# A shared ring of six small buffers for the key choice's maxima in a hybrid attention step

## The chip, the cores and the metric

The kernel runs on one core of a Trainium2 chip. The time is the device time of one execution in microseconds (us). Five engines work in parallel, each through its own queue in order: TensorE (PE, matmuls and transposes), VectorE (DVE), ScalarE (ACT), GpSimd (POOL) and SyncE (SP), which here only issues transfers. An instruction that waits holds up all that stand behind it in the queue of its engine.

## The reference

One step of a streaming encoder layer over 576 tokens: 512 of a prompt and 64 of a sample, which also sees 128 cached ones. The input is projected once; the columns belong to two groups of eight heads each. The first group is attention with a forget gate, the second is sparse attention: each query may only use the keys that an indexer chooses.

```python
def dsa_attend(q, k, v, iq, ik, iw, q_pos, k_pos, topk):
    logits = jnp.einsum('bqhd,bld->bqhl', iq, ik, preferred_element_type=jnp.float32)
    score = jnp.einsum('bqh,bqhl->bql', iw.astype(jnp.float32), jax.nn.relu(logits))
    admissible = (k_pos[None, :] // CHUNK) <= (q_pos[:, None] // CHUNK)
    score = jnp.where(admissible[None], score, NEG)
    _, sel = lax.top_k(score, topk)
    ...
    s = jnp.einsum('bqhd,bqkhd->bhqk', q, kg, preferred_element_type=jnp.float32) * HEAD_DIM ** -0.5
    p = jax.nn.softmax(jnp.where(valid[:, None], s, NEG), axis=-1)
```

`topk` is 128 for the prompt and 48 for the sample. Then come an output projection, a layer norm, a feed-forward part of width 4096 with a squared ReLU, a second layer norm, and a gated addition. All of it is in float32.

## The kernel before, in words

**Tiling.** Tokens lie along the free dimension, and 1024 features are eight tiles of 128 rows. Each float32 product is three matmuls of a rounded type, high by high, high by low and low by high; ACT makes the high half of every weight tile (L183), DVE or POOL the low half (L187). The heads are taken in eight pairs, 0 to 3 with the forget gate and 4 to 7 sparse. While the scores of pair p are worked off, PE projects pair p+1 (L279); both are mixed into one stream.

**Score jobs.** A pair has nine jobs: four blocks of 128 queries for each of two heads, with 128, 256, 384 and 512 keys, and one for the sample with both heads and 192 keys. A job runs through stages in successive ticks: `qk` (PE, L817, L824, L826) into a PSUM tile S; `addmax` (DVE, L834) adds the bias and takes the row's extreme into column 0 of a small tile `st`; `exp` (ACT, L842) reads it as its bias; for the sample job `norm` puts a sum and its reciprocal into `st` (L847, L848) and takes the reciprocal of the pair's sums (L850), which ACT spreads into `rows` (L852); `ptrans` transposes on PE; `pevac` copies to PT (ACT, L890, for pairs 0 to 3, DVE, L892, after that); `pv` (L912) multiplies with the values once for a whole pair. S, T and X share three PSUM banks, so a late reader of one of them stops PE.

**Key choice.** In pair 0 the indexer's logits are made (PE L611, ACT L616 into four buffers `work`, DVE L619 and L621 into `dbias`). A generator, `choice`, then runs rounds: the eight largest values of each row (`DVE.max`, L641) are replaced by a very small number (`match_replace`, L643, which the profile shows as a value load and a replacement). 16 rounds make 128 keys for each of the query blocks 1 to 3 (`dbias_97`, `dbias_98`, `dbias_99`, with 256, 384 and 512 keys), 6 rounds make 48 for the sample (`dbiasS`). An activation (L645) then turns what is left into a bias. Pair 4's jobs are the first that need it.

**What sets the order.** The source emits the instructions in one stream; after each step of the main loop a filler, `choose`, draws from `choice` at a fixed rate. The recording layer then reorders: an instruction may go ahead of earlier ones on its engine if its operands are ready by the layer's own estimate. A tile from a ring of `bufs` buffers can be written only after its buffer's last owner, `bufs` allocations ago in the source, has been read; so allocations of one ring stay in their order. The maxima lie in `m8`, one tile with two halves that rounds use in turn and that has no part in any ring. The statistics of the jobs lie in a ring `st` of four buffers.

Of the kernel before, what the change touches and what calls it, by code (L numbers as in the profile page):

```python
# [8 lines left out]
F32 = mybir.dt.float32  # L9
# [27 lines left out]
def tile_hybrid_step(ctx: ExitStack, tc: tile.TileContext, I, O):  # L37
# [249 lines left out]
    sb = pA.enter_context(tc.tile_pool(name="sb", bufs=1))  # L287
# [29 lines left out]
    cS = sb.tile([8, PAST + NS], F32, name="cS")  # L317
    dbiasS = sb.tile([128, PAST + NS], F32, name="dbiasS")
    iw = sb.tile([128, 5, 8], F32, name="iw")
    m8 = sb.tile([128, 2, 8], F32, name="m8")  # L320


    def tiles_of(name, k):
# [191 lines left out]
    def idx_rest():  # L515
        ACT.copy(ZkT[:, NP:NP + PAST], kiraw)
        DVE.tensor_tensor(ZkT[64:128, NP:NP + PAST], kiraw[64:128], f(ZkT[64:128, NP:NP + PAST]), OP.subtract)
        made = deque()
        for b0, nb in ((0, 2), (2, 2), (4, 1)):
            idx_rope(b0, nb)  # L520
            yield 1
            for b in range(b0, b0 + nb):
                for make, move in [zk_stack(b)] + ([zq_stack(b, hh) for hh in range(2)] if b else []):
                    make()
                    made.append(move)
                    if len(made) > 2:
                        made.popleft()()
                    yield 1
        done.add(0)
        while made:  # L530
            made.popleft()()
            yield 1
        SP.dma_start(O["ki"].rearrange("p (b d) -> p b d", b=5), idxs[:, :, 256:288])
# [68 lines left out]
    def logit_jobs():  # L602
        for i in range(1, 5):
            n, nk = (128, (i + 1) * 128) if i < 4 else (NS, PAST + NS)
            k0 = 0 if i < 4 else NP
            dst = dbias[i] if i < 4 else dbiasS
            while i not in done or (i < 4 and len(done) < i + 1):
                yield 0.5
            for h in range(8):
                ps = psum_1("SX"[h % 2], 1)  # L610
                PE.matmul(ps[:n, :nk], ZqT[:, h, (i - 1) * 128:(i - 1) * 128 + n], ZkT[:, k0:k0 + nk],  # L611
                          start=True, stop=True)
                r = work[:, h % 4 * 512:h % 4 * 512 + 512]

                def ev(h=h, n=n, nk=nk, i=i, ps=ps, r=r, dst=dst):
                    ACT.activation(r[:n, :nk], ps[:n, :nk], AF.Relu)  # L616
                    w = iw[:n, i, h:h + 1]
                    if h == 0:
                        DVE.tensor_scalar(dst[:n, :nk], r[:n, :nk], w, None, op0=OP.mult)  # L619
                    else:  # L620
                        DVE.scalar_tensor_tensor(dst[:n, :nk], r[:n, :nk], w, dst[:n, :nk], op0=OP.mult, op1=OP.add)  # L621
                later(LG, ev)
                yield nk / 960 + 0.1

    def choice():
        for _ in idx_rest():
            yield 0.6
        yield from logit_jobs()
        state["logits"] = True
        for _ in range(4):  # L630
            yield 0.5
        POOL.memset(dbias[0], 0.0)
        POOL.memset(dbias[0][0:64, 64:128], -NEG)
        for i in range(1, 5):
            n = 128 if i < 4 else NS
            s = dbias[i] if i < 4 else dbiasS[:NS]
            if i < 4:
                DVE.memset(s[0:64, i * 128 + 64:(i + 1) * 128], NEG)
            for r in range(16 if i < 4 else 6):
                m = m8[:n, r % 2]  # L640
                DVE.max(m, s)  # L641
                yield s.shape[1] / 960 + 0.1
                DVE.match_replace(out=s, in_to_replace=m, in_values=s, imm_value=GONE)  # L643
                yield s.shape[1] / 960 + 0.1
            ACT.activation(s, s, AF.Relu, bias=big[:n, 0:1])  # L645
            if i == 4:
                ACT.copy(dbiasS[64:128], dbiasS[0:64])
            state["chosen"] = i
            yield 0.4
# [179 lines left out]
    def addmax(j):  # L829
        n = j["S"].shape[1]  # L830
        t = sb.tile([128, 512], F32, name="sP", bufs=4)
        st = sb.tile([128, 4], F32, name="st", bufs=4)
        j["P"], j["st"] = t[:, :n], st
        DVE.tensor_tensor_reduce(j["P"], j["S"], j["bias"], scale=1.0, scalar=-GONE, op0=OP.add, op1=OP.min,  # L834
                                 accum_out=st[:, 0:1])
# [92 lines left out]
    def jobs_of(p):  # L928
        out = [dict(p=p, hh=hh, i=i, s=False, close=i % 2 == 1 and hh == 1) for i in range(4) for hh in range(2)]
        return out + [dict(p=p, s=True, close=True)]  # L930

    PLAN = (((oevac, 5), (addmax, 1), (exp, 2), (make_bias, 0), (make_bias, -1)),
            ((ptrans, 3), (norm, 2)),
            ((qk, 0), (pevac, 3), (scales, 3), (pv, 4)))
# [59 lines left out]
    drive(idx_main(), 24, None, 0)  # L994
    n_proj = 24
    state["choice"] = choice()
    bg = bg0()
    next(bg)
# [564 lines left out]
```

## Time and profile before

| What | Value |
|---|---|
| Median of three runs | 794.18 us (794.14 to 794.25) |
| Profiled execution, whole | 795.54 us |
| Its span, first to last instruction | 793.8 us |
| PE busy | 780.9 us, 98% |
| PE weight loads busy | 759.0 us, 96% |
| DVE busy | 539.4 us, 68%, 1100 instructions |
| ACT busy | 434.0 us, 55% |
| POOL busy | 119.4 us, 15% |
| Granted TensorE clock | 0.999 |
| MAX8 of the blocks, of the sample | 48 and 6 |

Busy times come from the profile's first part. A matmul's end is modelled, so PE's busy time is not PE at its peak. In a row of a timeline stand the start, the duration, the engine, the source line, the operation, the tiles written and read with their shapes, and in brackets the idle time ahead of it and who ended it. In a row of the view by stretches stand the stretch, its length, and busy time with instruction count for each engine.

### The profile page before, as it was taken

How to read it: one execution, taken by the hardware profiler on the slowest of the kernel's cores; microseconds unless marked ns; L12 is line 12 of the kernel's file. 1: busy time of each engine (PE TensorE's matmuls, PEld its weight loads, DVE VectorE, ACT ScalarE, POOL GpSimd, SP SyncE). 2: the span in 40 equal slices, each digit the busy share in tenths (PEclk: the TensorE clock that was granted, in tenths of full speed). 3: DMA queues.
4: the chain of work that ended last, by engine and by line, in shares of the span. 5: the costliest groups of instructions: out<-in, count | busy, mean ns of one | idle time of the engine just before them, and what ended most of it. 6: DMA issues, size and time to landing. Idle time of an engine off the chain costs nothing.

```text
span 793.8 us, 14800 instructions
## 1 busy us (share of the span) xinstructions
PE 780.9 (98%) x5822; PEld 759.0 (96%) x5822; DVE 539.4 (68%) x1100; ACT 434.0 (55%) x912; POOL 119.4 (15%) x121
## 2 busy tenths in 40 slices
PE   9999899999999999999999999999999999999997
PEld 8988798899999999999999999999999999999997
DVE  7679999653556655989846749477494765647653
ACT  5468666787777645587415426254362534626451
POOL 8103244454242000110000000000000000012200
PEclk9999999999999999999999999999999999999999
DMA  8537132344222233341214223042231413631001
GB/s 299 195 41 168 58 105 92 100 157 144 89 85 86 72 99 112 150 152 64 97 54 130 83 65 120 30 136 78 82 105 32 156 54 107 244 108 35 28 27 67
DMA packets 31127, 81.44 MB, mean 103 GB/s; under 512 B 5073, under 2 KB 10193, under 8 KB 30929
## 3 DMA queue, kind: packets, MB, share of 16 engines
q1 hardware_dynamic: 30768, 80.27, 31.8%
q8 instruction: 46, 0.75, 0.4%
q10 hardware_dynamic: 288, 0.22, 0.1%
q14 instruction: 25, 0.20, 0.1%
HBM read 66.38 MB, written 9.54 MB: 96 GB/s over the span
## 4 chain that ended last, share of the span: by engine, by line
PE 80%; DVE 10%; issue 5%; ACT 2%; POOL 1%; DMA 1%; SPq 0%; DVEq 0%; ACTq 0%; POOLq 0%
PE g L279 55%; PE m L279 13%; PE n L279 2%; DVE dbias L643 2%; DVE m L641 2%; PE V L912 2%; PE T L65 1%; DVE dbias L621 1%; PE m L422 1%; PE X L65 1%; PE m L429 1%; PE S L826 1%; PE S L429 1%; PE S L824 1%; DVE sP L834 1%
## 5 line engine op out<-in xcount | busy, mean ns | idle before, releaser
L183 ACT CAST whl<-wraw 128x512 fp32r<-128x512 f32 (+1 forms) x226 | 134.9, 611 | 168.9 <-PE g L279 145.1
L279 PE MATMUL g<-BH,whl 128*128 128x288 f32 (+2 forms) x864 | 181.6, 297 | 0.5 <-DVE Y L1218 0.5
L279 PE MATMUL m<-AH,whl 128*128 128x288 f32 x736 | 177.9, 308 | 0.0
L187 DVE TENSOR_TENSOR whl<-wraw,whl 128x512 fp32r<-128x512 f32 (+1 forms) x192 | 130.1, 697 | 68.2 <-ACT whl L183 67.4
L279 PEld LDWEIGHTS g<-BH,whl 128*128 128x128 f32 x864 | 141.1, 188 | 2.7 <-ACT u L1327 1.1
L279 PEld LDWEIGHTS m<-AH,whl 128*128 128x128 f32 x736 | 126.3, 188 | 1.9 <-issue 1.0
L279 PE MATMUL g<-BL,whl 128*128 128x288 f32 (+2 forms) x432 | 127.3, 295 | 0.0
L279 PE MATMUL m<-AL,whl 128*128 128x288 f32 x368 | 109.0, 296 | 0.0
L279 PE MATMUL g<-hidE,whl 128*128 128x288 f32 (+2 forms) x768 | 103.4, 295 | 0.0
L279 PE MATMUL g<-hidO,whl 128*128 128x288 f32 (+2 forms) x768 | 103.3, 295 | 0.0
L279 PEld LDWEIGHTS g<-hidO,whl 128*128 128x128 f32 x768 | 102.3, 188 | 0.0
L279 PEld LDWEIGHTS g<-hidE,whl 128*128 128x128 f32 x768 | 102.2, 188 | 0.1
L279 PEld LDWEIGHTS g<-BL,whl 128*128 128x128 f32 x432 | 81.3, 188 | 0.2
L279 PEld LDWEIGHTS m<-AL,whl 128*128 128x128 f32 x368 | 69.5, 189 | 0.7
L279 PE MATMUL g<-s,whl 128*128 128x288 f32 x432 | 68.4, 298 | 0.0
L279 PEld LDWEIGHTS g<-s,whl 128*128 128x128 f32 x432 | 60.0, 188 | 2.2 <-DVE u L1329 1.2
L1108 POOL TENSOR_TENSOR ln_s<-Y 128x576 f32<-128x576 f32 (+2 forms) x3 | 4.4, 1469 | 381.6 <-DVE Y L1393 369.2
L842 ACT ACTIVATE sP<-sP,st 128x128 f32<-128x128 f32 (+4 forms) x72 | 39.6, 550 | 35.4 <-DVE st L834 35.2
L187 POOL TENSOR_TENSOR whl<-wraw,whl 128x512 fp32r<-128x512 f32 x34 | 44.2, 1301 | 81.9 <-ACT whl L183 46.6
L1368 DVE SCALAR_TENSOR_TENSOR Y<-Y,g 128x576 f32<-128x576 f32 x48 | 36.0, 751 | 21.6 <-PE g L279 21.2
L279 PE MATMUL m<-BH,whl 128*128 128x288 f32 x192 | 43.4, 304 | 0.0
L183 ACT CAST whl<-wsum 128x512 fp32r<-128x512 f32 x24 | 14.8, 617 | 32.9 <-PE g L279 32.7
(282 smaller groups left out, 1263.9 us busy)
## 6 DMA issues: line engine op xcount, KB each, us to landing
wraw<-in_w_up_dram SPq DMA_DIRECT2D x32, 512.0 KB, 3.5
wraw<-in_w_down_dram SPq DMA_DIRECT2D x32, 512.0 KB, 3.5
wraw<-in_w_qkv_dram SPq DMA_DIRECT2D x23, 512.0 KB, 3.6
wraw<-in_w_gate_dram SPq DMA_DIRECT2D x8, 512.0 KB, 4.4
wraw<-in_w_o_dram SPq DMA_DIRECT2D x8, 384.0 KB, 3.1
out_vT_dram<-v SPq DMA_DIRECT2D x8, 288.0 KB, 2.1
Y<-in_xT_dram SPq DMA_DIRECT2D x8, 288.0 KB, 4.4
PLD<-PL SPq DMA_DIRECT2D x4, 576.0 KB, 3.5
```

The source lines that it names most:

```text
L65: PE.transpose(out, in_, ident[:n, :n])
L183: ACT.copy(self.hv[h][0], src)
L187: eng.tensor_tensor(lv, src, f(hv), OP.subtract)
L279: PE.matmul(ps, W(w, kw, wc), a[:, ka, cols], start=(first and i == 0), stop=(last and i == n - 1))
L422: PE.matmul(mk[:, h, :HW], w0(part, k), a[:, k, h * HW:(h + 1) * HW], start=(k == 0 and i == 0), stop=(k == 7 and i == 2))
L429: PE.matmul(acc[b][:n[b], :304], a[:, k, b * 128:b * 128 + n[b]], ixw(part, k), start=(k == 0 and i == 0), stop=(k == 7 and i == 2))
L621: DVE.scalar_tensor_tensor(dst[:n, :nk], r[:n, :nk], w, dst[:n, :nk], op0=OP.mult, op1=OP.add)
L641: DVE.max(m, s)
L643: DVE.match_replace(out=s, in_to_replace=m, in_values=s, imm_value=GONE)
L842: ACT.activation(j["P"], j["P"], AF.Exp, bias=j["st"][:, 0:1], scale=-1.0, accum_out=s)
L912: PE.matmul(P["O"][r, (i - 1) * 128 + c.start:(i + 1) * 128], P["vt"][:, kb, r], t[:, hh, kb, c], start=(kb == 0), stop=(kb == i))
L1368: later(0, lambda y=y, m=m, s=s: DVE.scalar_tensor_tensor(y, y, s, m[:, :, :HW], op0=OP.mult, op1=OP.add))
```

## The change

`m8` is gone. A round takes its maxima's tile from the ring `st`, whose tiles now have eight columns and of which there are six. Score jobs take theirs from the same ring. Nothing else is edited; below the edit, line numbers are 3 higher (L641 becomes L644, L834 becomes L837).

```diff
-    m8 = sb.tile([128, 2, 8], F32, name="m8")
...
+    def stats():
+
+        return sb.tile([128, 8], F32, name="st", bufs=6)
+
...
-                m = m8[:n, r % 2]
+                m = stats()[:n]
                 DVE.max(m, s)
...
-        st = sb.tile([128, 4], F32, name="st", bufs=4)
+        st = stats()
```

The order on PE and on POOL stays as it was. On DVE the rounds stand elsewhere. The first place is the end of pair 0 on DVE, where the last weighted sums of the logits (`dbiasS<-work`) are made; `ISA sP,st` is `addmax`, and `m_105` is the tile `m8`. Before:

```order
L621 SCALAR_TENSOR_TENSOR dbiasS<-work,iw,dbiasS 64x192
L643 MATCH_REPLACE dbias_97<-m_105,dbias_97 128x256
L621 SCALAR_TENSOR_TENSOR dbiasS<-work,iw,dbiasS 64x192
L850 RECIPROCAL sums<-sums 128x8
L641 MAX m_105<-dbias_97 128x8
L621 SCALAR_TENSOR_TENSOR dbiasS<-work,iw,dbiasS 64x192
L643 MATCH_REPLACE dbias_97<-m_105,dbias_97 128x256
L621 SCALAR_TENSOR_TENSOR dbiasS<-work,iw,dbiasS 64x192
```

Now:

```order
L620 SCALAR_TENSOR_TENSOR dbiasS<-work,iw,dbiasS 64x192 x2
L853 RECIPROCAL sums<-sums 128x8
L620 SCALAR_TENSOR_TENSOR dbiasS<-work,iw,dbiasS 64x192 x3
L837 ISA sP,st<-S,biasS 128x192
L837 ISA st 128x1
L620 SCALAR_TENSOR_TENSOR dbiasS<-work,iw,dbiasS 64x192
L850 RECIPROCAL st<-st 128x1
L837 ISA sP,st<-S,causal 128x128
L837 ISA st 128x1
L644 MAX st<-dbias_97 128x8
```

No round stands between the weighted sums any more; the first one comes behind pair 1's first job. The second place is DVE around the third job of pair 1, the first with 256 keys. Before:

```order
L834 ISA sP,st<-S,causal 128x128
L834 ISA st 128x1
L643 MATCH_REPLACE dbias_97<-m_105,dbias_97 128x256
L641 MAX m_105<-dbias_97 128x8
L641 MAX m_105<-dbias_98 128x8
L643 MATCH_REPLACE dbias_97<-m_105,dbias_97 128x256
L643 MATCH_REPLACE dbias_98<-m_105,dbias_98 128x384
L641 MAX m_105<-dbias_98 128x8
L834 ISA sP,st<-S,causal 128x256
```

Now:

```order
L644 MAX st<-dbias_97 128x8
L646 MATCH_REPLACE dbias_97<-st,dbias_97 128x256
L837 ISA sP,st<-S,causal 128x256
L837 ISA st 128x1
L644 MAX st<-dbias_97 128x8
L646 MATCH_REPLACE dbias_97<-st,dbias_97 128x256
L927 TENSOR_TENSOR mix_1357<-V,mix_1357 128x512
L837 ISA sP,st<-S,causal 128x256
```

Before, the 16 rounds of the 256 keys ended ahead of this job; now it stands behind six of them. The third place is DVE at the end of pair 3, with the rotary products of the next pair's queries (`x`, `xr`, `qE`, `qO`). Before:

```order
L834 ISA sP,st<-S,causal 128x512
L834 ISA st 128x1
L721 SCALAR_TENSOR_TENSOR x_2209<-m,cosT 128x576
L722 TENSOR_TENSOR xr<-xr,sinT 128x576
L723 TENSOR_TENSOR x_2209<-x_2209,xr 128x576
L834 ISA sP,st<-S,causal 128x512
L834 ISA st 128x1
L727 TENSOR_TENSOR qE<-x_2209,qE 64x576
L728 TENSOR_TENSOR qO<-x_2209,qO 64x576
L850 RECIPROCAL sums<-sums 128x8
L834 ISA sP,st<-S,biasS 128x192
```

Now:

```order
L837 ISA st 128x1
L724 SCALAR_TENSOR_TENSOR x_2248<-m,cosT 128x576
L725 TENSOR_TENSOR xr<-xr,sinT 128x576
L644 MAX st<-dbias_99 128x8
L726 TENSOR_TENSOR x_2248<-x_2248,xr 128x576
L646 MATCH_REPLACE dbias_99<-st,dbias_99 128x512
L837 ISA sP,st<-S,causal 128x512
L837 ISA st 128x1
L730 TENSOR_TENSOR qE<-x_2248,qE 64x576
L731 TENSOR_TENSOR qO<-x_2248,qO 64x576
L644 MAX st<-dbias_99 128x8
L853 RECIPROCAL sums<-sums 128x8
```

No round stood in pair 3 behind its second job; now the rounds of the 512 keys do, and the last rounds of the sample stand in pair 4, ahead of its seventh job.

## The prediction

> **What bounds the kernel now.** I read the chain of waits first, to see which engine the end hangs on.
>
> ```profile
> ## 4 chain that ended last, share of the span: by engine, by line
> PE 80%; DVE 10%; issue 5%; ACT 2%; POOL 1%; DMA 1%; SPq 0%; DVEq 0%; ACTq 0%; POOLq 0%
> ```
>
> TensorE (PE) carries most of it, but a tenth of the chain, some 79 us, lies on VectorE (DVE). The view by stretches shows where. I cut it at the starts of the value products of the head pairs, the 24 matmuls of L912, because they come once per pair:
>
> ```profile
> L912 PE MATMUL V<-PT,vtok x24: 272/379/430, 95.8 to 97.9; 128*64 128x256 f32 x16, 128*64 128x128 f32 x8
> L912 PE MATMUL V<-PT,vtok x24: 272/379/430, 126.3 to 128.4; 128*64 128x256 f32 x16, 128*64 128x128 f32 x8
> L912 PE MATMUL V<-PT,vtok x24: 272/379/430, 155.7 to 157.8; 128*64 128x256 f32 x16, 128*64 128x128 f32 x8
> L912 PE MATMUL V<-PT,vtok x24: 272/379/430, 184.0 to 186.1; 128*64 128x256 f32 x16, 128*64 128x128 f32 x8
> L912 PE MATMUL V<-PT,vtok x24: 272/379/430, 212.3 to 214.4; 128*64 128x256 f32 x16, 128*64 128x128 f32 x8
> ```
>
> ```profile
> core 0: us, PE busy (x) PEld busy (x) DVE busy (x) ACT busy (x) POOL busy (x), PEclk, DMA share, GB/s
> 60.00:86.00 26.00, 23.57 (x160) 21.32 (x159) 25.70 (x69) 21.67 (x58) 7.46 (x7) 1.00 0.55 128
> 86.00:95.80 9.80, 8.93 (x71) 8.32 (x68) 9.42 (x34) 4.51 (x14) 1.29 (x1) 1.00 0.26 85
> 95.80:126.30 30.50, 29.20 (x222) 27.24 (x221) 29.55 (x85) 19.55 (x51) 12.92 (x11) 1.00 0.34 101
> 126.30:155.70 29.40, 28.82 (x224) 27.30 (x223) 24.95 (x75) 21.33 (x55) 15.42 (x14) 1.00 0.35 105
> 155.70:184.00 28.30, 28.30 (x224) 27.20 (x223) 10.95 (x30) 24.09 (x58) 13.54 (x11) 1.00 0.51 169
> 184.00:212.30 28.30, 28.30 (x222) 27.23 (x221) 14.24 (x38) 21.39 (x50) 11.74 (x9) 1.00 0.27 91
> ```
>
> From 60 to 126 us DVE is busy 97 to 99% of the time, and PE takes 30.50 us for 222 matmuls that take it 28.30 us later. The next pair takes 29.40 us for the 224 that take 28.30 us after it. So a full DVE costs PE 2.2 and 1.1 us in these two steps. Before 95.8 us there is no undisturbed twin to compare with; PE's recorded idle time is 2.43 + 0.87 = 3.3 us. Altogether about 6.6 us of PE time are lost while the key choice runs, and from 155.7 us, when its rounds are over, nothing.
>
> Trace Analysis of the Trainium skill (Identifying the Most-Contended Engine) says that matmul busy time judges PE badly, because matmuls are pipelined, and weight-load busy time judges it better. By matmul busy time the two steps would lose only 1.30 + 0.58 = 1.9 us; by weight loads the share is 89% and 93% against 96% later, which is 3.2 us, and the trace's own step lengths side with that.
>
> The waits of PE themselves, in the timeline:
>
> ```profile
> 74.69 0.50 PE L824 MATMUL S<-kE,qE 128*128 128x512 f32 x1 [0.47 <-ACT PT L890]
> 84.76 0.59 PE L817 MATMUL S<-KcT,QB 128*128 128x192 f32 x2 [1.57 <-ACT PT L890]
> 94.35 0.39 PE L824 MATMUL S<-kE,qE 128*128 128x256 f32 x1 [0.56 <-DVE st L834]
> 95.17 0.66 PE L65 MATMUL X<-ident,rows 128*128 128x128 f32 x4 [0.31 <-ACT VS L774]
> 124.93 0.39 PE L824 MATMUL S<-kE,qE 128*128 128x256 f32 x1 [0.70 <-DVE st L834]
> ```
>
> Two name DVE. Those that name ScalarE (ACT) go back to DVE too, as the largest shows:
>
> ```profile
> 82.13 0.20 ACT L842 ACTIVATION_READ_ACCUMULATOR sP<-sP,st 128x1 f32 x1
> 83.50 0.18 DVE L850 RECIPROCAL sums<-sums 128x8 f32<-128x8 f32 x1
> 83.72 0.62 ACT L852 COPY rows<-sums 128x512 f32<-128x512 f32 x1 [0.97 <-DVE sums L850]
> ```
>
> The sums were ready at 82.33 us, the reciprocal ran 1.17 us later behind rounds and weighted sums, ACT's copy waited for it, and behind that copy in ACT's queue stood the copy of PT for which PE waited 1.57 us.
>
> **The change part by part.** Removed: one tile. Added: nothing that executes. The number of rounds is the same, 48 + 6, and PE's and POOL's orders are word for word the old ones apart from buffer numbers; on SP one load of Y passes one store. Moved: the rounds on DVE, and with them ACT's four activations and one copy that turn finished rounds into biases. One round is a MAX8, a value load and a MATCH_REPLACE8, and its pitch is the distance of two MAX8 with nothing between:
>
> ```profile
> 90.72 0.43 DVE L641 MAX8 m<-dbias 128x8 f32<-128x256 f32 x1
> 91.70 0.43 DVE L641 MAX8 m<-dbias 128x8 f32<-128x256 f32 x1
> 103.71 0.56 DVE L641 MAX8 m<-dbias 128x8 f32<-128x384 f32 x1
> 104.96 0.56 DVE L641 MAX8 m<-dbias 128x8 f32<-128x384 f32 x1
> 121.67 0.69 DVE L641 MAX8 m<-dbias 128x8 f32<-128x512 f32 x1
> 123.18 0.69 DVE L641 MAX8 m<-dbias 128x8 f32<-128x512 f32 x1
> ```
>
> So 0.98, 1.25 and 1.51 us for 256, 384 and 512 keys. A pair's jobs begin some 6 us before its step as cut above (89.53 for pair 1, below); I take the two as one. In the new order no round stands before pair 1's first score job; then some 16 + 2 rounds (256, 384) fall into pair 1, 14 + 1 (384, 512) into pair 2, 11.5 of 512 into pair 3, and the rest into pair 4.
>
> *The logit stage, 60 to 95.8 us.* In 60 to 86 us the two instructions of a round took, MAX8 first:
>
> ```profile
> 60.00:86.00 26.00, 3.32 (x8) 1.00 0.55 128
> 60.00:86.00 26.00, 3.82 (x16) 1.00 0.55 128
> ```
>
> That is 7.1 us of 26 that leave: DVE's 25.70 falls to 18.6. The 1.17 us of the late reciprocal go; of the 0.47 I count 0.2, because ACT's own queue has a part in it. The 0.56 at 94.35 came from this:
>
> ```profile
> 89.53 0.28 DVE L834 CUSTOM_DVE_ANT_0 sP<-S,causal 128x128 f32<-128x128 f32 x1
> 94.02 0.27 DVE L834 CUSTOM_DVE_ANT_0 sP<-S,causal 128x128 f32<-128x128 f32 x1
> 94.33 0.40 ACT L842 ACTIVATE sP<-sP,st 128x128 f32<-128x128 f32 x1 [3.02 <-DVE st L834]
> ```
>
> Between pair 1's first two score jobs 4.49 us of DVE work stood; now there are three rounds, 3 x 0.98 + 0.28 = 3.2 us. I count 0.5 of 0.56 and 0.2 of 0.31. Sum 2.1 us; bounds 1.2 (the reciprocal alone) and 3.3 (all recorded idle).
>
> *Pair 1, 95.8 to 126.3 us.* 16 x 0.98 + 2 x 1.25 = 18.2 us of rounds, and the other instructions take at most the 10.95 us of the third step, which has the rotary products on top: clearly under 29.2, where DVE held 29.55 before, and in narrow rounds, behind which a score job waits less. Of 2.2 us lost I count 1.9 back, bounds 1.1 and 2.2.
>
> *Pair 2.* 14 x 1.25 + 1.51 = 19.0 us of rounds in a step of 28.3, again beside 4 to 11 us. Of 1.1 lost, 0.8 back, bounds 0.4 and 1.1.
>
> *Pair 3, new load.* 11.5 x 1.51 = 17.4 us join 10.95 us: 28.3 of 28.3. Here DVE is full where it was 39% busy. The worst place is the pair's end, which ran like this:
>
> ```profile
> 168.85 0.69 DVE L834 CUSTOM_DVE_ANT_0 sP<-S,causal 128x512 f32<-128x512 f32 x1 [1.81 <-ACT whl L183]
> 171.91 0.69 DVE L834 CUSTOM_DVE_ANT_0 sP<-S,causal 128x512 f32<-128x512 f32 x1
> 175.28 0.20 DVE L850 RECIPROCAL sums<-sums 128x8 f32<-128x8 f32 x1 [1.04 <-ACT sP L842]
> 175.40 0.36 DVE L834 CUSTOM_DVE_ANT_0 sP<-S,biasS 128x192 f32<-128x192 f32 x1
> ```
>
> One round now stands between the first two rows, which have no idle time between them: the second comes 1.5 us late. One MAX8 (0.7) stands before the reciprocal and 1.04 us of idle absorb a part: 1.5 + 0.7 - 1.04 = 1.2 late. A MATCH_REPLACE8 and a MAX8 more (1.4) make the sample's job 2.6 late. Late by 3.0, the job at 94.02 cost PE 0.56; late by 1.17, the reciprocal at 83.50 cost 1.57, with a crowded ACT. I take a loss of 1.0 us, bounds 0 and 2.2 (all that a full step lost before). Pair 4 has about 3.5 x 1.51 + 6 rounds of 192 keys, near 10 us, beside 14.24: slack again.
>
> *The ring.* A MAX8 must now wait until the buffer's owner six allocations back has been read, for a score job by ACT's exponential; behind it queue the next scores, which ACT waits for. The longest such lag that I find with a busy ACT is this, 2.1 us from statistic to exponential:
>
> ```profile
> 97.38 0.08 DVE L834 DVE_READ_ACCUMULATOR2_ANT st<- 128x1 f32 x1
> 99.50 0.51 ACT L842 ACTIVATE sP<-sP,st 128x256 f32<-128x256 f32 x1
> ```
>
> Six allocations are one or two jobs and four or five rounds, at least 4 us of DVE work. I count zero; as a bound, see the second rival.
>
> *Sum:* -2.1 - 1.9 - 0.8 + 1.0 = -3.8 us, with PE full from 155.7 us on except near the end, so that nothing downstream takes it back. The profiled execution, 793.8 us of span and 795.54 us in all, becomes about 791.7; the median of the runs, 794.18, is 1.4 below it and becomes 790.4.
>
> **The rivals.** *ACT takes DVE's place.* Two of PE's waits name ACT, which is busy 83% in 60 to 86 us; freed from DVE's lateness, PE would meet ACT. Then the logit stage gives 0.5, pair 1 1.0, pair 2 0.4, and pair 3 still costs 1.0: -0.9, 793.3 us, no change. Against it: in 155.7 to 184.0 us ACT is busy 85% (24.09) and PE never idles.
>
> *The ring closes a loop, and it is slower.* If ACT is later than the 4 us of work between two owners, MAX8 waits for the exponential, the next score job waits behind MAX8, and the next exponential for that job. Each pair's lateness then lasts. Pairs 1 to 4 would each lose what the fullest step lost, 4 x 2.2 = 8.8, against 3.3 now, while the logit stage still returns 2.1: +3.4, 797.6 us. It decides from a lag of 4 us; the trace shows 2.1. For it speaks that pair 3 has no slack to recover in.
>
> That the rounds do not move is excluded by the order.
>
> **How the numbers follow.** Two runs of this kernel can be told apart from about 0.2%, 1.6 us. Forecast 0.73, ACT as the bound 0.15, the loop 0.12. The forecast's terms at their bounds give -6.6 (787.6) and -1.2 - 1.1 - 0.4 + 2.2 = -0.5 (793.7). The low end I put at 787.2. Upward the range takes in the ACT case and stops at 794.8, short of the loop. Faster 0.73, since most of the forecast's own range lies under 792.6; same 0.15; slower 0.12.
>
> **What would show it.** Right: the distances between L912 groups are near 28.5 us for pairs 1 and 2, PE's idle time in 60 to 96 us falls to about 1.2 us, the 1.57 us wait is gone, the last round stands in pair 4, after 184 us, and DVE in the third step rises to 28 us with PE waits under 1 us in all. ACT as bound: PE's waits before 126 us stay and name ACT while DVE shows idle time. The loop: idle DVE before MAX8, released by ACT's exponential. I am wrong if a step after 155.7 us grows by more than 1 us, or if 60 to 126 us does not shrink.

## The result, and the profile after

The change takes 789.47 us, the median of six runs (789.1 to 790.71), against 794.22 us for the kernel before in the same rounds (794.14 to 795.82). The ratio is 0.994, 95% interval 0.993 to 0.995: faster by more than the 0.2% that can be told from no change, and 0.9 us under the forecast of 790.4. The profiled execution takes 790.67 us with a span of 788.9 us, 4.9 us less than that of before. Executions of one kernel mostly fall into two lengths, some 1.6 us apart, which arise in the first 10 us (last section): like with like the change gains 5.0 to 5.1 us (794.2 to 789.2, 795.8 to 790.7), the two profiles compared here both have the longer start, and most of those further down have the shorter one, so distances between cuts are compared there.

The chain of waits of the kernel after, shares of the span by engine:

```profile
PE 90%; DVE 5%; ACT 2%; issue 1%; DMA 1%; POOL 0%; DVEq 0%; SPq 0%; ACTq 0%
```

DVE's part of the chain is halved, and the shares for "issue" and POOL shrank; PE has gained them. The value products, now at L915, give the cuts again:

```profile
L915 PE MATMUL V<-PT,vtok x24: 272/379/430, 94.0 to 96.1; 128*64 128x256 f32 x16, 128*64 128x128 f32 x8
L915 PE MATMUL V<-PT,vtok x24: 272/379/430, 122.3 to 124.4; 128*64 128x256 f32 x16, 128*64 128x128 f32 x8
L915 PE MATMUL V<-PT,vtok x24: 272/379/431, 150.7 to 152.8; 128*64 128x256 f32 x16, 128*64 128x128 f32 x8
L915 PE MATMUL V<-PT,vtok x24: 272/379/430, 179.0 to 181.1; 128*64 128x256 f32 x16, 128*64 128x128 f32 x8
L915 PE MATMUL V<-PT,vtok x24: 272/379/430, 207.4 to 209.5; 128*64 128x256 f32 x16, 128*64 128x128 f32 x8
```

The view by stretches at these cuts, kernel after:

```profile
core 0: us, PE busy (x) PEld busy (x) DVE busy (x) ACT busy (x) POOL busy (x), PEclk, DMA share, GB/s
60.00:86.00 26.00, 24.23 (x164) 21.83 (x162) 22.73 (x48) 21.96 (x59) 7.17 (x8) 1.00 0.56 131
86.00:94.00 8.00, 8.00 (x65) 7.83 (x63) 6.33 (x25) 5.17 (x15) 2.55 (x2) 1.00 0.25 93
94.00:122.30 28.30, 28.30 (x222) 27.25 (x221) 22.24 (x74) 19.47 (x51) 12.90 (x11) 1.00 0.38 109
122.30:150.70 28.40, 28.40 (x224) 27.27 (x223) 22.57 (x65) 19.48 (x51) 14.16 (x13) 1.00 0.37 108
150.70:179.00 28.30, 28.30 (x222) 27.21 (x221) 25.14 (x63) 23.96 (x58) 13.55 (x11) 1.00 0.55 171
179.00:207.40 28.40, 28.40 (x224) 27.28 (x223) 18.32 (x57) 22.85 (x53) 11.82 (x10) 1.00 0.29 89
```

Set against the rows of before, the stage up to the first cut is 1.8 us shorter (95.8 to 94.0), pair 1's step 2.2 us (30.5 to 28.3), pair 2's 1.0 us (29.4 to 28.4), and pair 3's has the same length although DVE works 25.14 us in it in place of 10.95. From 86 us on PE is busy in every stretch for its whole length. All of the gain, 5.0 us, is there at 179.0 us.

Of PE's waits between 55 and 210 us the timeline has two left:

```profile
78.31 0.30 PE L610 MATMUL X<-Z 128*64 128x192 f32 x1 [0.18 <-ACT work L615]
84.00 0.30 PE L610 MATMUL X<-Z 128*64 128x192 f32 x1 [1.20 <-ACT work L615]
```

The 1.57 us wait is gone, but 1.20 us stand almost at its place. The timeline of all engines tells why (an "x2" joins two instructions in a row):

```profile
80.95 1.28 POOL L187 TENSOR_TENSOR whl<-wraw,whl 128x512 fp32r<-128x512 f32 x1 [5.67 <-DVE st L837]
81.13 1.82 DVE L620 SCALAR_TENSOR_TENSOR dbiasS<-work,iw,dbiasS 64x192 f32<-64x192 f32 x2 [0.25 <-ACT work L615]
81.82 0.20 ACT L845 ACTIVATION_READ_ACCUMULATOR sP<-sP,st 128x1 f32 x1
82.88 0.19 DVE L853 RECIPROCAL sums<-sums 128x8 f32<-128x8 f32 x1
83.06 0.41 DVE L620 SCALAR_TENSOR_TENSOR dbiasS<-work,iw,dbiasS 64x192 f32<-64x192 f32 x1
83.10 0.62 ACT L855 COPY rows<-sums 128x512 f32<-128x512 f32 x1 [0.87 <-DVE sums L853]
83.62 0.32 ACT L615 ACTIVATE work<-X 64x192 f32<-64x192 f32 x1
```

The sums are ready at 82.02 us. The reciprocal is still 0.86 us late, now behind two weighted sums that take 1.82 us together where one alone takes 0.41; a subtraction on POOL runs at the same time. ACT's copy waits 0.87 us for the reciprocal, and the activation behind it frees the bank X for which PE waits.

Where the rounds went, by the view of the two lines that make them:

```profile
L644 DVE MAX8 st<-dbias x48: 418/556/695, 87.4 to 176.6; 128x8 f32<-128x256 f32 x16, 128x8 f32<-128x384 f32 x16, 128x8 f32<-128x512 f32 x16
L646 DVE MATCH_REPLACE8 dbiasS<-st,dbiasS x6: 333/334/335, 179.6 to 189.1; 64x192 f32<-64x192 f32 x6
```

The first stands at 87.4 us, behind pair 1's first job, and the last ends in pair 4. The end of pair 3 on DVE:

```profile
167.75 0.68 DVE L837 CUSTOM_DVE_ANT_0 sP<-S,causal 128x512 f32<-128x512 f32 x1
170.86 0.20 DVE L853 RECIPROCAL sums<-sums 128x8 f32<-128x8 f32 x1
172.32 0.34 DVE L837 CUSTOM_DVE_ANT_0 sP<-S,biasS 128x192 f32<-128x192 f32 x1
```

Take 5.0 us, by which everything here stands earlier, from the old 171.91, 175.28 and 175.40, and these three are late by 0.8, 0.6 and 1.9 us. PE waited for none of them.

### The profile page after: what moved, and what is told of

It is laid out like the page before. It is cut to its first block, busy times and chain, and to the rows that moved or that the text cites. A ratio compares the mean times of both kernels' runs of the same rounds, so it can differ in the third digit from the quotient of the medians.

```text
span 788.9 us, 14810 instructions
## 1 busy us (share of the span) xinstructions
PE 779.4 (99%) x5822; PEld 759.1 (96%) x5822; DVE 540.9 (69%) x1100; ACT 434.5 (55%) x912; POOL 119.0 (15%) x121
## 4 chain that ended last, share of the span: by engine, by line
PE 90%; DVE 5%; ACT 2%; issue 1%; DMA 1%; POOL 0%; DVEq 0%; SPq 0%; ACTq 0%
PE g L279 55%; PE m L279 20%; PE n L279 2%; PE T L65 2%; PE V L915 2%; DVE dbias L620 1%; PE S L829 1%; PE S L827 1%; PE X L65 1%; PE m L421 1%; PE m L428 1%; PE S L428 1%; DVE whl L187 1%; DMA xraw<-in_xT_dram 0%; DMA wraw<-in_w_up_dram 0%
```

## The experiments

All ratios are to the kernel before in the same rounds (794.2 to 794.3 us each time), with 95% intervals.

**Is it the sharing, the six buffers, or the waiting?** Three kernels. The first is the kernel before with the jobs' statistics alone in a ring of six:

```diff
-        st = sb.tile([128, 4], F32, name="st", bufs=4)
+        st = sb.tile([128, 8], F32, name="st", bufs=6)
```

> The kernel before, with the score jobs' ring at six tiles of eight columns; the rounds keep their own m8, and the order on every engine is that of before. If the gain is the place of the rounds: 794.2 us, no change against before. If the wider ring of the jobs is what helps (a score job waits less for a free st): 789 to 791 us.

The second is the change with a ring of six that belongs to the rounds alone:

```diff
-                m = stats()[:n]
+                m = sb.tile([128, 8], F32, name="mx", bufs=6)[:n]
```

> The changed kernel, but the maxima come from a ring of six of their own, which the jobs do not share. The rounds then stand where they stood before. If sharing is what places them: 794.2 us. If a ring for the maxima as such is enough (six tiles in place of two halves, fewer waits from round to round): about 789.5 us.

The third keeps the sharing, with four buffers, so that a maximum waits for an owner two allocations nearer:

```diff
-        return sb.tile([128, 8], F32, name="st", bufs=6)
+        return sb.tile([128, 8], F32, name="st", bufs=4)
```

> The changed kernel with four tiles in the shared ring in place of six; the order on every engine is that of the change. If only the order counts: 789.5 us, the same as the change, with no idle time of DVE before a MAX8. If the ring closes a loop through ACT's exponential (the second rival of the prediction), four tiles must show it: idle time before MAX8 named ACT, and 791 us or more.

Measured: 794.2 us (ratio 0.9997, 0.9987 to 1.0006), 794.86 us (1.0003, 0.9993 to 1.0012) and 789.21 us (0.9936, 0.9922 to 0.9951). The view by stretches, first of the kernel with the rounds' own ring:

```profile
94.30:124.90 30.60, 29.32 (x224) 27.34 (x223) 29.64 (x86) 19.64 (x52) 12.89 (x11) 1.00 0.34 101
124.90:154.20 29.30, 28.72 (x224) 27.23 (x223) 24.88 (x74) 21.26 (x54) 15.44 (x14) 1.00 0.38 105
```

and of the shared ring of four:

```profile
93.70:122.00 28.30, 28.30 (x222) 27.21 (x222) 22.37 (x74) 19.44 (x51) 12.95 (x11) 1.00 0.37 109
122.00:150.30 28.30, 28.30 (x222) 27.25 (x221) 22.23 (x65) 19.30 (x51) 14.20 (x13) 1.00 0.36 109
```

With a ring of their own the rounds stand where they stood in the kernel before, and the time is the old one. With a shared one they stay where the source has them, with four buffers as with six. The number of buffers does nothing; that rounds and jobs draw from one sequence does all. And a ring two shorter does not wait: DVE has no idle time before a MAX8, so the loop through ACT's exponential, which would have closed sooner with four, is not there.

**Is it the stage that is relieved, or DVE's fill afterwards?** Here the change stays, but once the logits are done the filler draws rounds faster than 0.63 per step:

```diff
-        state["k"] += state["rate"]
+        state["k"] += 1.0 if state["logits"] else state["rate"]
```

> The changed kernel with the filler's rate at 1.0 in place of 0.63 once the logits are done: no round in the logit stage, but pairs 1 and 2 hold as many rounds as DVE can take, and the last ends early in pair 3. It parts the logit stage's share from that of pairs 1 and 2. If a full DVE costs PE some 2.2 and 1.1 us in these steps: 789.5 + 3 = about 792.5 us, with the distances of the value products back at 30 and 29.4. If the gain came from the logit stage alone and the steps lost for another reason: 789.5.

Measured: 794.15 us, 0.9999 (0.999 to 1.0008). The whole gain is gone, which no term of mine had allowed. The view by stretches of this kernel:

```profile
92.80:122.40 29.60, 28.78 (x224) 27.22 (x223) 28.22 (x89) 19.32 (x49) 13.29 (x12) 1.00 0.35 104
122.40:154.10 31.70, 29.98 (x222) 27.36 (x221) 30.70 (x83) 20.31 (x52) 14.18 (x13) 1.00 0.33 97
```

The first cut stands at 92.8 us, 1.5 us earlier than the 94.3 of the own ring, so the logit stage keeps its gain. The next two steps take 29.6 + 31.7 = 61.3 us against 30.6 + 29.3 = 59.9 there: 1.4 us are given back, and both kernels reach the next cut at about the same time. It looks as if what counts is when DVE has worked off its backlog: while it is 95 to 97% busy, PE goes at DVE's pace, and time won ahead of that is waited away in it. Why 1.3 us are lost in the one step and 3.3 in the other was not separated; ACT's exponentials wait for DVE's statistics 5.3 us in the first and 9.2 us in the second.

Two rates between, 0.8 and 0.9 in place of 1.0:

> The changed kernel with the filler's rate at 0.8 once the logits are done (the change has 0.63, dense_pairs had 1.0 and lost the whole gain). PE's order is that of the change; pair 1 now holds 16 rounds of 256 and some 6 of 384 keys, pair 2 the other 10 and 4 of 512. By busy time that is 22.2 + 5 = 27 of 28.3 us in pair 1. If PE loses only where DVE's work exceeds the step: 789.5, at most 790.3. If each score job's lateness behind more rounds counts by itself: halfway, 791 to 792.

> As rate_08, with 0.9: about 3 more rounds in pair 1, so that DVE has some 30 us of work in a step of 28.3, and it stays full until the rounds end in pair 3. If DVE's work beyond the step is what PE pays: 791.5 to 793. If a full DVE costs nothing until rounds stand densely ahead of single jobs: 789.5 to 790.3.

Measured: 789.88 us, 0.9943 (0.9928 to 0.9958), and 791.54 us, 0.9967 (0.9956 to 0.9979). The view by stretches at rate 0.8:

```profile
92.40:120.80 28.40, 28.40 (x224) 27.29 (x223) 26.34 (x85) 19.43 (x52) 12.69 (x11) 1.00 0.36 108
120.80:149.40 28.60, 28.47 (x222) 27.21 (x221) 26.28 (x71) 19.09 (x51) 13.91 (x14) 1.00 0.36 108
```

and at 0.9:

```profile
92.50:121.80 29.30, 28.98 (x225) 27.32 (x223) 27.75 (x89) 18.64 (x49) 11.68 (x10) 1.00 0.36 105
121.80:150.90 29.10, 28.72 (x222) 27.25 (x221) 28.17 (x74) 19.61 (x51) 15.40 (x14) 1.00 0.36 106
150.90:179.90 29.00, 28.67 (x224) 27.35 (x223) 16.84 (x53) 26.29 (x62) 13.90 (x11) 1.00 0.47 159
```

With DVE 92 to 93% busy a step is 0.1 to 0.3 us over 28.3, at 95 to 97% it is 0.8 to 1.0 over, and in the kernel before and at rate 1.0 up to 3.4. The last row at 0.9 shows that the mean of a step is not the whole measure: DVE is 58% busy over it, but the last rounds stand at its beginning, and 0.7 us are lost.

**What do the rounds still cost?** None are run, so that every admissible key is kept, which changes the output:

```diff
-            for r in range(16 if i < 4 else 6):
+            for r in range(0):
```

> The changed kernel without any round (the choice then keeps every admissible key, which changes the output); all else stays, with the same order on PE. It gives the floor. If the rounds now cost nothing, since PE has no idle time from 94 to 207 us: 789.3 us, within 0.5 of the change. If they still cost something that the idle times do not show: 787 to 788.

Measured: 789.19 us, 0.9938 (0.9924 to 0.9953), the time of the change. View by stretches:

```profile
92.50:120.80 28.30, 28.30 (x222) 27.25 (x221) 6.05 (x23) 18.95 (x50) 12.90 (x11) 1.00 0.36 109
120.80:149.20 28.40, 28.40 (x224) 27.28 (x223) 6.15 (x24) 19.09 (x50) 14.15 (x13) 1.00 0.37 108
```

Where the change keeps DVE busy for 22.24 us, this one does for 6.05, and PE's step is 28.30 us in both. The 54 rounds now cost nothing; what is left to win in this region lies in the logit stage.

**Does pair 3 stand at the edge?** Each of the last 14 rounds of the 512 keys gets a second search for maxima, into a tile that nobody reads:

```diff
+    spare = sb.tile([128, 2, 8], F32, name="spare")
...
+                if i == 3 and r > 1:
+                    DVE.max(spare[:, r % 2], s)
```

> The changed kernel with 14 more MAX8 of 512 keys, one before each of the last 14 rounds of block 3, into a tile that nobody reads: 14 x 0.72 = 10 us more on DVE, 7 of them in pair 3, where it is busy 25.1 of 28.3 us. It asks why pair 3's new load cost 0 us and not the 1.0 predicted. If PE loses time only where DVE's work exceeds the step: 25.1 + 7 = 32, so some 3 to 4 us in pair 3's step and up to 2 in pair 4's, 793 to 795 us. If lateness behind single rounds counts even with DVE full for a while, more than that; if the jobs have slack to hide even this: 789.5.

Measured: 791.65 us, 0.9965 (0.9952 to 0.9978), less of a loss than expected. View by stretches:

```profile
149.10:178.80 29.70, 28.75 (x218) 26.76 (x217) 29.12 (x66) 23.90 (x55) 14.10 (x11) 1.00 0.50 164
178.80:208.30 29.50, 29.50 (x228) 27.92 (x227) 20.93 (x65) 23.55 (x56) 11.71 (x9) 1.00 0.27 84
```

Three of the searches already stand in the step ahead, which keeps its length of 28.3 us; ten stand in pair 3's step and one in pair 4's. These 11 x 0.69 = 7.6 us of DVE work, and what they push back, cost the two steps 29.7 + 29.5 - 28.3 - 28.4 = 2.5 us; the rest filled slack of this pair (DVE from 25.14 to 29.12 us) and of the next (18.32 to 20.93). So pair 3 of the change is close to the edge, but below it.

**What holds the logit stage?** A flag at the planner of the weight tiles (L330) gives the low halves of a unit to POOL. Two more units go to DVE:

```diff
-            U[kind, p] = WT.add(qkv[p * 3 + x], pool_l=(p * 3 + x > 6))
+            U[kind, p] = WT.add(qkv[p * 3 + x], pool_l=(p * 3 + x > 8))
```

> The changed kernel with the low halves of weight units 7 and 8, four subtractions of 128x512, on DVE in place of POOL. In the logit stage a weighted sum on DVE (two tiles of SBUF in) takes 1.31 us in place of 0.41 while POOL subtracts, and behind it PE's last wait of 1.2 us builds up. If POOL's subtraction blocks it: the long sums go (4 x 0.9 us), DVE gains 4 x 0.67 us of work, PE's 1.2 us wait shrinks by about 0.9: 788.6 us. If the sums are long for another reason: DVE is 2.7 us fuller in a stage of 26, and the time is 789.5 to 790.5.

Then the second of the two alone, with `p * 3 + x > 6 and p * 3 + x != 8`:

> As the last, but only unit 8's two low halves go to DVE; the one that POOL made from 80.95 to 82.23 us ran beside the long sum ahead of the late reciprocal. If POOL blocks DVE there: 788.6 us and the 1.2 us wait smaller by 0.9 at 1.3 us more of DVE work. Else 789.5 to 790.

Measured: 787.47 us, 0.9912 (0.9897 to 0.9927), and 789.35 us, 0.9939 (0.9923 to 0.9956). The first beats both kernels. It was not timed in the same rounds as the change, but the two intervals to the kernel before (0.9897 to 0.9927, 0.993 to 0.995) do not meet, its four runs lie between 787.43 and 787.48 us where the change's six begin at 789.1, and against the kernel without rounds, which was timed in the same rounds, it gains 1.7 us (787.47 to 789.19), with the first cut at 90.7 us in place of 92.5. The second gains 0.7 us at the first cut (91.8), and its median decides nothing. The logit stage without rounds, which has the same start and, like the change, no round in this stretch, and with both units on DVE:

```profile
60.00:86.00 26.00, 24.37 (x164) 21.86 (x164) 21.86 (x48) 23.46 (x62) 8.28 (x8) 1.00 0.53 137
60.00:86.00 26.00, 25.15 (x179) 23.64 (x179) 23.23 (x58) 22.82 (x61) 2.17 (x4) 1.00 0.60 152
```

POOL has lost four subtractions (8.28 to 2.17 us), DVE has ten instructions more (21.86 to 23.23 us), and PE does 179 matmuls in place of 164. The weighted sums, minimum, median and maximum in ns, first in the change:

```profile
L620 DVE SCALAR_TENSOR_TENSOR dbias<-work,iw,dbias x21: 479/618/1600, 54.9 to 78.7; 128x256 f32<-128x256 f32 x7, 128x384 f32<-128x384 f32 x7, 128x512 f32<-128x512 f32 x7
L620 DVE SCALAR_TENSOR_TENSOR dbiasS<-work,iw,dbiasS x7: 408/410/1311, 79.9 to 85.7; 64x192 f32<-64x192 f32 x7
```

then with both units on DVE:

```profile
L620 DVE SCALAR_TENSOR_TENSOR dbias<-work,iw,dbias x21: 480/619/752, 53.4 to 75.7; 128x256 f32<-128x256 f32 x7, 128x384 f32<-128x384 f32 x7, 128x512 f32<-128x512 f32 x7
L620 DVE SCALAR_TENSOR_TENSOR dbiasS<-work,iw,dbiasS x7: 404/410/412, 76.9 to 82.4; 64x192 f32<-64x192 f32 x7
```

The medians are the same and the long ones are gone: DVE's sums were stretched by up to about 0.9 us each while POOL subtracted. With unit 8 alone moved, whose subtractions stood beside the narrow sums, only these are short again: their maximum is 412 ns, that of the wide ones still 1590. PE has no recorded wait for a low half in the change, so the gain is not that these come sooner from DVE. Is this an independent gain? The same flag in the kernel before:

> The kernel before with the low halves of weight units 7 and 8 on DVE, as in pool_less (which gained 2.0 us on the changed kernel). In the kernel before DVE is full from 60 to 151 us. If PE then goes at DVE's pace, only DVE's total work counts: 4 x 0.67 us come, some 4 x 0.9 us of sums held up by POOL go, -0.9 us: 793.3, near no change. If POOL's hold on single sums is what PE waits for in both kernels: 792.2, the same 2 us.

Measured: 793.54 us, 0.9992 (0.9983 to 1.0002), no difference that can be told. The kernel before has DVE full up to 151 us, and the relief of the logit stage is worth little there, as it was at rate 1.0: the first cut comes at 94.3 us in place of 95.8, but the next two steps take 30.7 + 30.3 = 61.0 us in place of 30.5 + 29.4 = 59.9. Last, five `work` buffers on top of the version with both units on DVE, against the one wait that it has left:

```diff
-                r = work[:, h % 4 * 512:h % 4 * 512 + 512]
+                c = ((i - 1) * 8 + h) % 5 * 512
+                r = work[:, c:c + 512]
```

> pool_less (787.5 us) with five buffers of logits in place of four, so that ACT waits less for a free one. What is left in the logit stage is one wait of PE, 0.73 us, for ACT's copy of PT behind the copy of the sums. If a free logit buffer is what delays ACT there: 787.0. If not: 787.5, no change against pool_less; in either case below the change by 2.

Measured: 787.7 us, 0.9915 (0.99 to 0.993), the same time as without. The wait of PE for ACT's copy to PT, 0.73 us at 81.02 us with four buffers, is 0.74 us at 81.05 us with five. So the four buffers did not cause it; its cause is not settled.

## Why the prediction was right or wrong

**The mechanism was right in the main.** PE lost its time where DVE was full or had just been. With the rounds spread, steps 1 and 2 have the 28.3 and 28.4 us forecast as "near 28.5", the last round stands in pair 4, and nothing downstream takes the gain back. That the cause is the order of the rounds, not the buffers or waits, is shown by the own ring and the shared ring of four.

Pair 2 sets a limit to it. Over its step in the kernel before DVE was 85% busy, not full: the view by stretches parts the step into one with 97% and a tail with 21%, and PE's recorded idle time, 0.57 us, lies in the tail.

```profile
126.30:151.00 24.70, 24.70 (x193) 23.61 (x192) 23.97 (x71) 16.96 (x43) 14.13 (x13) 1.00 0.35 104
151.00:155.70 4.70, 4.12 (x33) 3.69 (x31) 0.98 (x5) 4.37 (x12) 1.28 (x1) 1.00 0.37 112
151.41 0.44 ACT L645 ACTIVATE dbiasS<-dbiasS,big 64x192 f32<-64x192 f32 x1
151.88 0.35 ACT L647 COPY dbiasS<-dbiasS 64x192 f32<-64x192 f32 x1
152.26 0.58 ACT L769 COPY vtok<-X 128x512 f32<-128x512 f32 x1
```

PE waits there for ACT's copy into vtok, which stands in ACT's queue behind the instructions that turn the sample's finished rounds into biases. The change moves these too, so about half of pair 2's 1.1 us may have been ACT's part of the key choice and not DVE's; no run parts the two.

**The logit stage**: -2.1 forecast, -1.8 measured. PE's idle time from 60 us to the first cut fell from 3.3 to 26.00 - 24.23 = 1.8 us, not to 1.2. I had taken all of the 1.17 us by which the reciprocal was late as removed; 0.86 us of it stayed, since weighted sums stretched beside POOL took the place of the rounds. DVE's 25.70 us fell to 22.73 and not to 18.6: the 7.1 us of rounds left, and 4.1 us of other busy time stand in their place. Weighted sums are 1.9 us of it: 21 of them kept DVE busy for 13.59 us in this stretch, 22 now for 15.46, mostly by stretching. Some 0.3 us are the sample's score job, which the stretch now reaches. The rest is overlap: by their own durations DVE's instructions took some 30 us in the 25.70 busy ones, so that taking off the rounds' own 7.1 us took off too much.

**Pairs 1 and 2**: -1.9 and -0.8 forecast, -2.2 and -1.0 measured, their upper bounds but for 0.1 us. The discount for rounds that stand ahead of a score job was not needed. The weight-load rule of the Trainium skill, Perfetto Trace Analysis (Identifying the Most-Contended Engine), gave 3.2 us lost in these two steps where matmul busy time gave 1.9; the two came back with 30.5 + 29.4 - 28.3 - 28.4 = 3.2 us, and weight loads are now busy 96% of each step. The rule holds here.

**Pair 3** is the term that was mis-sized: +1.0 forecast, 0 measured. The step that failed is "17.4 us join 10.95 us: 28.3 of 28.3". The 10.95 was right (10.94 us without rounds), but the rounds add 25.14 - 10.94 = 14.2 us: 11 of them, at 1.29 us and not 1.51. The distance of two MAX8, by which I priced a round, is too much for two reasons: the round's own instructions take 7.60 + 8.22 = 15.8 us for the 11, or 1.44 us each, and some 0.15 us of that overlaps with neighbours, by about 0.08 us at each change of instruction (the score job at 167.75 us starts before the replacement of 167.15 us, which takes 0.68, has ended). The lateness at the pair's end was sized 1.5, 1.2 and 2.6 us and came out as 0.8, 0.6 and 1.9. That a full DVE would have cost there is shown by the doubled searches: 2.5 us over two steps at 29.12 of 29.70.

**The sum** was -3.8 and became -5.0: +0.3 in the logit stage, -0.3 and -0.2 in pairs 1 and 2, and -1.0 in pair 3, by far the largest error. Its form does not hold in general: it adds terms as if each stage kept its gain. With rate 1.0 the stage kept 1.5 us at the first cut and the kernel won nothing. The gains add here only because no step after the stage has DVE over 90% busy.

**The rivals.** ACT does not take DVE's place: from 86 us PE is busy throughout, with ACT at 69 to 85% of a step. The one larger wait that names ACT goes back to DVE and POOL, and moving POOL's work took it away; of ACT itself at most the 0.73 us of the last version can be meant. The loop of the ring does not close with six buffers nor with four.

## What to carry to other kernels

Read a helper engine's load by stretches, not over the span: at 68% of the span DVE cost PE most of 5 us in stretches where it was 95 to 99% busy, and steps with 92% and less lost almost nothing unless the work was bunched. Spread such work until no stretch is full, since a gain ahead of a full stretch is waited away in it. Where a recording layer may hoist work, a ring of buffers shared with its consumers pins it to the source's order: look at the order that comes out, and at what a helper's helper (POOL here) does to the instructions beside it.

## What was not expected of the hardware

**POOL holds up DVE's operations with two tensor inputs in SBUF.** A weighted sum of 64x192 takes 0.41 us, but 1.31 us beside a POOL subtraction of 1.28 us, and the wide ones reach 1.60 us; with four of the subtractions moved away the maxima are 0.41 and 0.75 us. MAX8, with one tensor input, is not stretched: at most 0.695 us while POOL is busy 13.55 of 28.3 us. Nor is an operation whose second tensor lies in PSUM: a rotary product takes its usual 0.76 us from 153.49 us on, beside a POOL subtraction from 152.81 to 154.10. And POOL can be the one that is held up: a cast of 0.60 us takes 1.19 us from 165.19 us on, beside a DVE product of two SBUF tensors that began at 165.15. The Trainium skill, SBUF — State Buffer (SBUF: two separate sides), says that DVE and GpSimd share one port pair as an exclusive lock, that on DVE's side this concerns, among others, operations with two SBUF inputs against a GpSimd operation that reads SBUF, and that the loser blocks fully. The durations agree with it, and moving the subtractions to DVE was worth 1.7 us.

**The start has two lengths.** The first 10 us of the profile of before, and a matmul in them:

```profile
0.00:10.00 10.00, 8.28 (x33) 7.51 (x34) 5.55 (x6) 4.48 (x9) 7.18 (x24) 1.00 0.80 271
...
7.50 0.46 PE L429 MATMUL m<-iw,AL 128*128 128x304 f32 x1
```

The same in the version with both units on DVE, whose first 10 us are not edited:

```profile
0.00:10.00 10.00, 8.29 (x42) 7.55 (x43) 6.09 (x7) 5.53 (x12) 7.73 (x25) 1.00 0.80 270
...
7.32 0.30 PE L428 MATMUL m<-iw,AL 128*128 128x304 f32 x1
```

Matmuls of one shape take 0.46 us until about 10.5 us in the one and until 7.3 us in the other: 33 against 42 in the same time, while the granted clock reads 1.00 in both. A third profile, of the kernel before with two units moved, shows the clock: there a matmul of this shape takes 0.30 us at 6.94 us, 0.46 us from 7.37 to 10.19, and 0.30 again from 10.86, and the row of the slow part reads half:

```profile
8.00:10.00 2.00, 2.00 (x10) 1.97 (x10) 2.00 (x5) 1.98 (x5) 0.52 (x2) 0.50 1.03 405
```

So 0.46 us is what such a matmul takes at half the clock, and a reading of 1.00 in the first 10 us does not exclude that. The Trainium skill, TensorE: Matmul & The Clock Gate (Part 1: The HAM clock gate), has the array at half speed until a window of about 3.4 us has been busy, and the window running freely, so that the count varies from run to run. The size agrees: matmuls become fast 3.2 us later here. No run tested the cause, and it is not the only one: in the longer start of the shared ring of four PE waits 1.47 us for DVE's low half of the input, and has fast matmuls from 8.55 us on.
